# Two weight units multiplied side by side while the input arrives, a zeroed tile multiplied first, and index queries for positions 128 to 511 only

## The chip, the cores and the metric

The kernel runs on one core of a Trainium2 chip. The metric is the device time of one execution in microseconds, as the median of several runs. One execution was also recorded by the hardware profiler, and all rows below come from that one.

## What is computed

A decoder trunk of two layers over one sequence of 512 positions and 1024 features, in float32. Cut to what matters for the change, which sits in the first stage of the first layer:

```python
h = x @ w_in                                 # one combined projection
q_a, c_kv, q_idx, k_idx, w_idx, q_b, k_b, v_b, f_in = _split(h, EVEN_WIDTHS)
q_idx = q_idx.reshape(bsz, seq, 8, 64) * (64 ** -0.5)
log_f = log_sigmoid(f_in + b_f); cum_f = jnp.cumsum(log_f, axis=1)
# per block of 128 query positions:
idx = jnp.einsum('bthd,bsd->bths', qi, k_idx)
score = jnp.einsum('bth,bths->bts', wi, relu(idx))
score = jnp.where(causal, score, -inf)
_, sel = lax.top_k(score, k_sel)             # k_sel = 128 keys for each query
# 8 sparse heads attend to the chosen keys, 8 forgetting heads to all earlier keys;
# then output projection, norm, ConvFFN, norm; a second layer of another kind follows
```

A query at position t sees only the keys up to t, so the first 128 positions choose among at most 128 keys and need no scores.

## The kernel before

**Numbers.** Every float32 operand of a product is held as two float32r parts, `hi` and `lo`, whose sum is the float32 value: ScalarE (ACT) casts it to `hi`, VectorE (DVE) subtracts to get `lo`. A product is then three matmuls (`mm3`, lines 147 to 151): hi by hi, hi by lo, lo by hi.

**Weights.** They stream from DRAM in the order of use as 192 units of [128, 1024], 512 KB each (class `Stream`, lines 41 to 88). SyncE (SP) issues the loads into three `raw` buffers; line 75 casts on ACT and line 76 subtracts on DVE into one of three `whi`/`wlo` pairs, or into a `quad` tile where one is registered. `get(i)` also splits the two units that follow. A `raw` buffer is loaded again only after line 76 has read it, and a `whi`/`wlo` pair is written again only after the last matmul that reads it.

**The first stage.** `xq` holds the transposed input as eight pieces k of [128, 512]. Lines 121 to 134 load weight unit 0 whole, then the eight pieces of 256 KB each, and cut every piece (lines 130 and 131). Unit 0 (index keys, forget gates, index weights) is multiplied with `proj` (line 341): 8 pieces by 3 matmuls of 512 columns, 24 in all. Its evacuation on ACT and DVE follows, with the forget gates behind it (lines 343 to 359). Units 1 to 4 give the index queries (lines 364 to 369): 24 matmuls of 512 columns each, and two cuts per unit on 64 partitions. Unit 5 gives the latent keys (line 381).

**Scores and choice.** `scores(j)` for j = 1, 2, 3 (lines 410 to 426) multiplies the query columns from 128 on with the index keys: 48 matmuls, each pair followed by a Relu on ACT and an accumulation into `sel[j]` on DVE. The rounds that choose 128 keys (`choose`, lines 428 to 441) are 48 DVE rounds of MAX8 and MATCH_REPLACE8. Manual dependencies place them behind certain DVE instructions, so they are spread over the value projection (lines 452 to 457), the pairs of forgetting heads and the heads themselves. Their last result, line 440 for j = 3, goes through GpSimd (POOL, line 441 and lines 526 to 537) into the biases of the sparse heads.

**Order.** The kernel is written with a tile framework whose planner orders each engine's instructions by dependencies and by a modelled time, not strictly by the program text. For instance the split of unit 3 stands on ACT ahead of line 343.

## Time and profile before

| | us |
|---|---|
| median of 3 runs | 1188.16 |
| lowest and highest run | 1186.97, 1189.46 |
| span of the profiled execution | 1186.8 |
| TensorE matmul (PE) busy in the span | 1164.2 (98%) |
| DVE busy | 720.6 (61%) |
| ACT busy | 472.3 (40%) |

The profiled execution's own time is its span of 1186.8 us and what lies around it, the start and the end of the program; the median of the runs is 1.4 us above the span, and that difference is carried over unchanged. A PE busy share says little by itself, because matmuls overlap: their starts are closer together than their durations. The distance between starts is what is read below.

### The profile page before, as it was taken

How to read it: one execution, taken by the hardware profiler on the slowest of the kernel's cores; microseconds unless marked ns; L12 is line 12 of the kernel's file. 1: busy time of each engine (PE TensorE's matmuls, PEld its weight loads, DVE VectorE, ACT ScalarE, POOL GpSimd, SP SyncE). 2: the span in 40 equal slices, each digit the busy share in tenths (PEclk: the TensorE clock that was granted, in tenths of full speed). 3: DMA queues.
4: the chain of work that ended last, by engine and by line, in shares of the span. 5: the costliest groups of instructions: out<-in, count | busy, mean ns of one | idle time of the engine just before them, and what ended most of it. 6: DMA issues, size and time to landing. Idle time of an engine off the chain costs nothing. (4 is left out here: it accounts for less than half of the span.)

```text
span 1186.8 us, 14493 instructions
## 1 busy us (share of the span) xinstructions
PE 1164.2 (98%) x5512; PEld 966.4 (81%) x5512; DVE 720.6 (61%) x1216; ACT 472.3 (40%) x749; POOL 151.8 (13%) x238
## 2 busy tenths in 40 slices
PE   7999999899999999999999999999999999999997
PEld 6887777788988888888888788888888888888885
DVE  6889987847565656552236864466655666552226
ACT  6616666732434344441233342232444443432121
POOL 1033634203000000000002300003000000010003
PEclk9999998999999999999999999999999999999999
DMA  6633201242123232343344223471232323344221
GB/s 220 206 93 128 89 9 46 95 137 89 54 93 103 91 105 89 107 142 121 128 142 135 87 89 118 137 242 72 71 107 89 102 93 97 116 142 142 89 89 71
DMA packets 39685, 129.89 MB, mean 109 GB/s; under 512 B 5096, under 2 KB 5104, under 8 KB 39616
## 3 DMA queue, kind: packets, MB, share of 16 engines
q1 hardware_dynamic: 34560, 113.26, 29.0%
q0 software_dynamic: 5056, 15.71, 4.1%
q8 instruction: 43, 0.70, 0.3%
q14 instruction: 26, 0.21, 0.1%
HBM read 120.54 MB, written 9.99 MB: 110 GB/s over the span
## 5 line engine op out<-in xcount | busy, mean ns | idle before, releaser
L76 DVE TENSOR_TENSOR wlo<-raw,whi 128x1024 fp32r<-128x1024 f32 x161 | 197.3, 1226 | 290.7 <-ACT whi L75 289.6
L149 PE MATMUL bank<-quad,whi 128*128 128x512 f32 (+1 forms) x932 | 356.6, 383 | 6.3 <-ACT quad L130 6.3
L150 PE MATMUL bank<-quad,whi 128*128 128x512 f32 (+1 forms) x932 | 355.8, 382 | 0.5 <-DVE quad L131 0.5
L151 PE MATMUL bank<-quad,wlo 128*128 128x512 f32 (+1 forms) x932 | 355.9, 382 | 0.0
L75 ACT CAST whi<-raw 128x1024 fp32r<-128x1024 f32 x161 | 169.5, 1053 | 261.7 <-PE bank L151 120.6
L149 PEld LDWEIGHTS bank<-quad,whi 128*128 128x128 f32 x932 | 175.5, 189 | 40.2 <-ACT quad L130 6.3
L150 PEld LDWEIGHTS bank<-quad,whi 128*128 128x128 f32 x932 | 175.8, 189 | 34.6 <-DVE quad L131 1.1
L151 PEld LDWEIGHTS bank<-quad,wlo 128*128 128x128 f32 x932 | 175.7, 188 | 33.8
L150 PE MATMUL bank<-wlo,quad 128*128 128x512 f32 x388 | 151.0, 389 | 0.0
L151 PE MATMUL bank<-whi,quad 128*128 128x512 f32 x388 | 150.7, 389 | 0.0
L149 PE MATMUL bank<-whi,quad 128*128 128x512 f32 x388 | 149.5, 389 | 0.0
L149 PE MATMUL bank<-quad 128*128 128x512 f32 (+5 forms) x280 | 99.8, 360 | 0.5 <-ACT quad L187 0.5
L150 PE MATMUL bank<-quad 128*128 128x512 f32 (+5 forms) x280 | 98.7, 353 | 0.6 <-DVE quad L76 0.6
L151 PE MATMUL bank<-quad 128*128 128x512 f32 (+5 forms) x280 | 98.6, 353 | 0.0
L206 POOL DMA_DIRECT2D temp<-x x24 | 13.2, 549 | 567.9 <-ACT quadx L317 424.6
L150 PEld LDWEIGHTS bank<-wlo,quad 128*128 128x128 f32 x388 | 72.8, 188 | 15.2
L149 PEld LDWEIGHTS bank<-whi,quad 128*128 128x128 f32 x388 | 72.8, 188 | 15.1
L151 PEld LDWEIGHTS bank<-whi,quad 128*128 128x128 f32 x388 | 72.8, 188 | 14.9
L286 DVE SCALAR_TENSOR_TENSOR temp<-bank,fcw,temp 128x511 f32<-128x511 f32 x88 | 65.5, 744 | 9.1 <-ACT temp L285 9.1
L288 DVE SCALAR_TENSOR_TENSOR temp<-bank,fcw,temp 128x510 f32<-128x510 f32 x88 | 65.9, 748 | 3.0
L285 ACT ACTIVATE temp<-bank,fcw 128x512 f32<-128x512 f32 x88 | 59.9, 681 | 10.8 <-PE bank L151 10.8
L313 ACT ACTIVATE temp<-temp 128x512 f32<-128x512 f32 x44 | 27.8, 632 | 88.5 <-DVE temp L288 88.5
(143 smaller groups left out, 1274.2 us busy)
## 6 DMA issues: line engine op xcount, KB each, us to landing
raw<-in_ws_dram SPq DMA_DIRECT2D x192, 512.0 KB, 3.5
x<-temp SPq DMA_DIRECT2D x24, 256.0 KB, 2.0
temp<-x POOLq DMA_DIRECT2D x24, 256.0 KB, 3.2
temp<-in_xT_dram SPq DMA_DIRECT2D x8, 256.0 KB, 6.0
temp<-fk_d SPq DMA_DIRECT2D x8, 256.0 KB, 4.8
temp<-in_x_dram POOLq DMA_DIRECT2D x8, 256.0 KB, 3.1
quad<-in_ln_g_dram POOLq DMA_DIRECT2D x4, 512.0 KB, 5.2
quad<-in_ln_b_dram POOLq DMA_DIRECT2D x4, 512.0 KB, 6.6
```

Of the source, the lines that this page charges most:

```text
L75: nc.scalar.copy(hi, t)
L76: dve[0] = nc.vector.tensor_tensor(out=lo, in0=t, in1=_f(hi), op=ALU.subtract)
L149: nc.tensor.matmul(out, a[0], b[0], start=first, stop=False)
L150: nc.tensor.matmul(out, a[0], b[1], start=False, stop=False)
L151: return nc.tensor.matmul(out, a[1], b[0], start=False, stop=last)
L206: nc.gpsimd.dma_start(t, src[n * 128:n * 128 + 128, hf * 512:hf * 512 + 512])
L285: nc.scalar.mul(t, p, cw[:, j, 2:3])
L286: nc.vector.scalar_tensor_tensor(out=t[:, 1:], in0=p[:, :S - 1], scalar=cw[:, j, 1:2], in1=t[:, 1:], op0=ALU.mult, op1=ALU.add)
L288: nc.vector.scalar_tensor_tensor(out=t[:, 2:], in0=p[:, :S - 2], scalar=cw[:, j, 0:1], in1=t[:, 2:], op0=ALU.mult, op1=ALU.add)
L313: nc.scalar.activation(tg, tg, AF.Silu)
```

## The change

- A quad `misc` is taken first, and DVE sets its first [128, 512] part to zero. TensorE begins with 7 matmuls of 512 columns on that zero tile, whose result nobody reads (`WARM`).
- Units 0 and 1 are loaded directly, each in two halves of 256 KB (`load_w`), in among the eight input pieces: unit 0 first half, piece 0, unit 1 first half, pieces 1 to 3, unit 0 second half, piece 4, unit 1 second half, pieces 5 to 7. Each half is cut by itself.
- The two units are multiplied together, piece by piece: for each k three matmuls of unit 0 (512 columns) and three of unit 1.
- The index queries (units 1 to 4) are computed for columns 128 to 511 only: matmuls of 384 columns instead of 512, and cuts of 384 columns.
- Later units run through `Stream` as before. The evacuation of unit 0 with the gates follows the joint products, and the call that splits units 2, 3 and 4 stands in the program text behind it.

```diff
+    misc = quad()
     xq = [[quad(), quad()], [quad(), quad()]]
-    ws.load_to(1)
+    nc.vector.memset(_f(misc[:, 0]), 0.0)
+    w0 = [(rawp.tile([128, 1024], F32, name="raw"), wp.tile([128, 1024], FR, name="whi"),
+           wp.tile([128, 1024], FR, name="wlo")) for _ in range(FIRST)]
+    def load_w(u, hf):
+        c = slice(hf * 512, hf * 512 + 512)
+        raw, hi, lo = (t[:, c] for t in w0[u])
+        nc.sync.dma_start(raw, A["ws"][u][:, c])
+        nc.scalar.copy(hi, raw)
+        nc.vector.tensor_tensor(out=lo, in0=raw, in1=_f(hi), op=ALU.subtract)
...
+    load_w(0, 0)
+    load_x(0)
+    load_w(1, 0)
+    for k in (1, 2, 3):
+        load_x(k)
+    load_w(0, 1)
+    load_x(4)
+    load_w(1, 1)
+    for k in (5, 6, 7):
+        load_x(k)
+    ws.loaded = ws.split_to = base[0] = FIRST
...
-        misc = quad()
-        w = unit()
-        p = proj(w, xq)
+        q = bank()
+        for _ in range(WARM):
+            nc.tensor.matmul(q, misc[:, 0, :128], misc[:, 0], start=True, stop=True)
+        p0 = [bank() for _ in range(FIRST)]
+        for k in range(8):
+            for u in range(FIRST):
+                a = 128 if u else 0
+                w = w0[u][1:]
+                mm3(p0[u][:, a:], wk(w, k * 128, k * 128 + 128), xk(xq, k, a), k == 0, k == 7)
+        p = p0[0]
...
+        late_q = slice(128, S)
         for m in range(4):
-            p = proj(unit(), xq)
+            if m < FIRST - 1:
+                p = p0[1 + m]
+            else:
+                p = bank()
+                half(unit(), xq, p, 128, S)
             for s, (a, b) in enumerate(((slice(0, 64), slice(64, 128)), (slice(64, 128), slice(0, 64)))):
-                nc.scalar.mul(qi[s][a, m], p[a], float(HD ** -0.5))
+                nc.scalar.mul(qi[s][a, m, late_q], p[a, late_q], float(HD ** -0.5))
...
```

## Rows read from the trace of the kernel before

**Rows 1.** The page: the span, and the busy time, share and instructions of four engine rows (PE matmuls, PEld weight loads).

```profile
span 1186.8 us, 14493 instructions
...
PE 1164.2 (98%) x5512; PEld 966.4 (81%) x5512; DVE 720.6 (61%) x1216; ACT 472.3 (40%) x749; POOL 151.8 (13%) x238
```

**Rows 2.** The waits of TensorE over the whole run: who waited for whom, total us, times, longest us. The four longest.

```profile
PE bank L149 <- ACT quad L130: 6.3, 1, 6.3
PE bank L149 <- ACT pt L187: 3.5, 4, 1.4
PE bank L150 <- DVE pt L188: 1.2, 1, 1.2
PE bank L600 <- DVE d L590: 1.1, 1, 1.1
```

**Rows 3.** The timeline of TensorE from 0 to 52 us: start us, duration us. The first product, three at the first pitch, the first at another pitch, the first product of unit 1 and of unit 2, and the first scores.

```profile
6.34 0.80 PE L149 MATMUL bank<-quad,whi 128*128 128x512 f32 x1 [6.34 <-ACT quad L130]
...
8.27 0.63 PE L151 MATMUL bank<-quad,wlo 128*128 128x512 f32 x1
...
8.70 0.63 PE L149 MATMUL bank<-quad,whi 128*128 128x512 f32 x1
...
11.26 0.54 PE L149 MATMUL bank<-quad,whi 128*128 128x512 f32 x1
...
14.82 0.39 PE L149 MATMUL bank<-quad,whi 128*128 128x512 f32 x1
...
20.28 0.39 PE L149 MATMUL bank<-quad,whi 128*128 128x512 f32 x1
...
43.67 8.62 PE L416 MATMUL bank<-quad 128*128 128x256 f32 x48
```

**Rows 4.** The timeline of SP and ACT from 0 to 40 us: the issue of unit 0's load on SP; on ACT unit 0's cast, the casts of the input pieces (8 in three groups), the casts of units 2 and 3, the evacuation of unit 0 and the last instruction of its gates.

```profile
0.80 0.39 SPq L59 DMA_DIRECT2D raw<-in_ws_dram  x1
...
4.72 1.04 ACT L75 CAST whi<-raw 128x1024 fp32r<-128x1024 f32 x1 [2.64 <-DMA raw<-in_ws_dram]
5.67 1.13 ACT L130 CAST quad<-temp 128x512 fp32r<-128x512 f32 x2
...
10.17 1.96 ACT L130 CAST quad<-temp 128x512 fp32r<-128x512 f32 x3 [0.25 <-DMA temp<-in_xT_dram]
...
14.07 1.06 ACT L75 CAST whi<-raw 128x1024 fp32r<-128x1024 f32 x1 [0.23 <-DMA raw<-in_ws_dram]
15.63 1.06 ACT L75 CAST whi<-raw 128x1024 fp32r<-128x1024 f32 x1 [0.51 <-DMA raw<-in_ws_dram]
16.59 0.57 ACT L343 COPY temp<-bank 128x512 f32<-128x512 f32 x1
...
21.23 0.63 ACT L354 ACTIVATE temp<-temp 8x512 f32<-8x512 f32 x1
```

**Rows 5.** The timeline of DVE from 0 to 40 us: its last instruction before the input arrives, two groups of input cuts, the cut of unit 3, the first cut of unit 0's result, and a memset of 512 columns.

```profile
0.90 0.07 DVE L143 MEMSET mhalf<- 128x8 f32 x1
...
6.94 1.29 DVE L131 TENSOR_TENSOR quad<-temp,quad 128x512 fp32r<-128x512 f32 x2
...
10.83 2.04 DVE L131 TENSOR_TENSOR quad<-temp,quad 128x512 fp32r<-128x512 f32 x3 [0.17 <-ACT quad L130]
...
16.72 1.23 DVE L76 TENSOR_TENSOR wlo<-raw,whi 128x1024 fp32r<-128x1024 f32 x1 [0.34 <-ACT whi L75]
17.87 0.68 DVE L345 TENSOR_TENSOR quad<-bank,quad 64x512 fp32r<-64x512 f32 x1
...
22.74 0.48 DVE L356 MEMSET temp<- 8x512 f32 x1 [0.16 <-DVE temp L355]
```

**Rows 6.** The timeline of TensorE in the heads' stage, where matmuls of 384 columns stand in a row: the first of three, and the first of 512 columns behind them.

```profile
113.49 0.34 PE L149 MATMUL bank<-quad 64*128 64x384 f32 x1
...
114.02 0.39 PE L149 MATMUL bank<-quad 64*128 64x512 f32 x1
```

**Rows 7.** Busy time by stretch, all engines: start and end in us, length, busy us of PE, PEld, DVE, ACT, POOL with instruction counts, granted clock, DMA share, GB/s. The first two lines are two stretches of the input's loading (pieces of 2 KB a partition, then whole units of 4 KB), the next two the stretches up to and through the choice of keys, the last two the stretches at a low granted clock.

```profile
6.00:10.00 4.00, 3.12 (x7) 2.13 (x8) 3.55 (x6) 2.62 (x5) 0.00 (x0) 1.00 1.03 349
11.00:13.50 2.50, 2.50 (x12) 2.04 (x11) 1.86 (x3) 1.79 (x3) 0.00 (x0) 1.00 1.03 418
...
16.70:80.40 63.70, 63.70 (x294) 52.79 (x293) 52.39 (x103) 32.79 (x59) 11.65 (x25) 1.00 0.45 148
80.40:183.50 103.10, 103.10 (x538) 81.59 (x538) 95.77 (x251) 62.04 (x154) 40.36 (x84) 1.00 0.25 82
...
192.20:199.00 6.80, 6.80 (x27) 5.36 (x26) 4.63 (x16) 3.50 (x12) 1.59 (x3) 0.52 0.15 60
236.60:240.00 3.40, 3.40 (x17) 3.18 (x16) 1.98 (x3) 1.71 (x2) 0.00 (x0) 0.54 0.47 158
```

**Rows 8.** The instructions of DVE from 15 to 45 us by line and shape (count, busy us, mean ns, idle before them), the line that cuts the index queries.

```profile
L368 DVE SCALAR_TENSOR_TENSOR quad<-bank,quad 64x512 fp32r<-64x512 f32 x8 | 5.5, 689 | 1.5 <-ACT quad L367 1.3
```

**Rows 9.** The instructions of line 440, the last comparison of each choice of keys: their durations in ns, first and last start in us.

```profile
L440 DVE TENSOR_TENSOR sel<-temp,sel x3: 424/540/693, 79.2 to 183.5; 128x256 f32<-128x256 f32 x1, 128x384 f32<-128x384 f32 x1, 128x512 f32<-128x512 f32 x1
```

**Rows 10.** The waits from 178 to 202 us: who waited for whom, total us, times, longest us.

```profile
POOL sel L441 <- DVE sel L440: 6.3, 1, 6.3
...
DVE d L572 <- POOL d L535: 2.1, 2, 1.6
```

More of the change, by code (lines that the diff above doesn't have):

```diff
@@ L31 @@
 S1, S2, S3, S4 = 4, 3, 1, 2
+WARM = 7
 def _f(ap):
@@ L118, in unit, with load_x @@
         return ws.get(i)
+    FIRST = 2
+    misc = quad()
     xq = [[quad(), quad()], [quad(), quad()]]
-    ws.load_to(1)
-    def load_x(c):
-        for j in range(2):
-            r = temp()
-            k = 2 * c + j
-            nc.sync.dma_start(r, A["xT"][:, k])
-            hi, lo = xq[0][k // 4][:, k % 4], xq[1][k // 4][:, k % 4]
-            nc.scalar.copy(hi, r)
-            nc.vector.tensor_tensor(out=lo, in0=r, in1=_f(hi), op=ALU.subtract)
-    for c in range(4):
-        load_x(c)
+    nc.vector.memset(_f(misc[:, 0]), 0.0)
[7 more added lines that the diff above has]
+        nc.vector.tensor_tensor(out=lo, in0=raw, in1=_f(hi), op=ALU.subtract)
+    def load_x(k):
+        r = temp()
+        nc.sync.dma_start(r, A["xT"][:, k])
+        hi, lo = xq[0][k // 4][:, k % 4], xq[1][k // 4][:, k % 4]
+        nc.scalar.copy(hi, r)
+        nc.vector.tensor_tensor(out=lo, in0=r, in1=_f(hi), op=ALU.subtract)
+    load_w(0, 0)
[9 more added lines that the diff above has]
+    ws.loaded = ws.split_to = base[0] = FIRST
     ident = cst.tile([128, 128], F32)
@@ L359, in _body @@
         nc.gpsimd.dma_start(fk_d, cw[g])
-        for k in range(5, 9):
-            ws.big[base[0] + k] = quad
+        for k in range(6, 10):
+            ws.big[k] = quad
         qi = [quad(), quad()]
+        late_q = slice(128, S)
         for m in range(4):
-            p = proj(unit(), xq)
+            if m < FIRST - 1:
[3 more added lines that the diff above has]
+                half(unit(), xq, p, 128, S)
             for s, (a, b) in enumerate(((slice(0, 64), slice(64, 128)), (slice(64, 128), slice(0, 64)))):
-                nc.scalar.mul(qi[s][a, m], p[a], float(HD ** -0.5))
-                nc.vector.scalar_tensor_tensor(out=qi[s][b, m], in0=p[a], scalar=float(HD ** -0.5),
-                                               in1=_f(qi[s][a, m]), op0=ALU.mult, op1=ALU.subtract)
+                nc.scalar.mul(qi[s][a, m, late_q], p[a, late_q], float(HD ** -0.5))
+                nc.vector.scalar_tensor_tensor(out=qi[s][b, m, late_q], in0=p[a, late_q], scalar=float(HD ** -0.5),
+                                               in1=_f(qi[s][a, m, late_q]), op0=ALU.mult, op1=ALU.subtract)
         p = bank()
```

## The prediction

> **What bounds the kernel now.** I read the page first: TensorE's matmuls are busy 98% of a span of 1186.8 us, DVE 61%, ACT 40% [rows 1]. Overlapping matmuls make such a share too kind, so I read TensorE's waits next: the largest is 6.3 us, once, for the first input piece, and the next three come to 5.8 us together [rows 2]. So TensorE seldom waits, and what it is spared early should reach the end, unless another engine then comes last.
>
> The starts of its matmuls give the price of a product. Unit 1's first product starts at 14.82 and unit 2's at 20.28 [rows 3]: 24 products of 512 columns in 5.46 us, 0.2275 us each, which is little over 512 columns at 2.4 GHz (0.213). The first products were slower: 8.27 to 8.70 is 0.43 us, 512 columns at 1.2 GHz, and the distance changes only in the product that starts at 11.26 [rows 3]. The engine began at 6.34 and was fed without a gap from 8.27. So the first stage has three losses: TensorE has nothing until 6.34, runs at half speed until 11.3, and spends 5.46 us on each index-query unit, a quarter of it on columns that no score reads.
>
> The third reading is the choice of keys. Its last comparison starts at 183.5 [rows 9]; POOL waits 6.3 us for it, DVE 2.1 us for POOL [rows 10], and TensorE 1.1 us for DVE [rows 2], and a stretch at a granted clock of about half follows, 6.8 us long [rows 7]. From 80.4 to 183.5 DVE is busy 95.77 of 103.1 us, 93% [rows 7]. So DVE's stream is the second bound, and it is nearly as tight as TensorE's.
>
> **Part 1: the joint start.** The arrival of data decides first. Unit 0, 512 KB, was there at 4.72; the last group of three pieces began to be cast at 10.17 and took 1.96 us [rows 4], so the last piece was there by 11.5. Its lo part was done at 12.87 [rows 5]. The pieces, 2 KB a partition, moved at 349 GB/s [rows 7]. With 256 KB first, the first half of unit 0 is there about 0.75 us sooner, at 4.0; piece 0 follows 0.75 us later, at about 4.9 with the queue, and its cast takes some 0.6 us (two in 1.13) [rows 4]. First product at 5.5, the second 0.7 us later (the lo cut, two in 1.29 us [rows 5]). Piece 7 has 512 KB more ahead of it, 1.3 to 1.5 us at 418 or 349 GB/s [rows 7]: there at 12.8, cast by 13.4, cut by 14.1.
>
> The work for TensorE is 24 products at 0.2275 and 24 of 384 columns. For the latter the nearest rows are those of the heads: three in a row from 113.49 to 114.02, 0.177 us each, on 64 rows [rows 6]; in proportion to 512 columns it is 0.171. I take 0.174. Together 5.46 + 4.18 = 9.6 us, 1.2 us per piece, against an arrival of 0.75 us per transfer and twelve transfers: from the second product on TensorE is the later one. At full clock: 6.2 + 9.4 = 15.6, and 0.2 for the cold part: 15.8. The arrival alone would allow 14.1 plus five products, 15.0.
>
> The clock: the zeroed tile takes DVE one memset, 0.48 us for 512 columns [rows 5], from about 0.95, so the seven products can start at 1.45 and last 7 x 0.43 = 3.0 us, to 4.5. Nothing in the trace shows how much of that counts. Before, the clock rose 4.9 us after the first product of any kind [rows 3]; the same distance from 1.45 gives 6.4. The bounds: at once at 4.5, or as if there had been no zero products, 5.5 + 4.9 = 10.4. In the second case some 4.4 us of work run at half speed, 2.2 us lost. So the joint products end at 15.7 to 17.9, I take 16.0, where unit 2 began at 20.28: **4.3 us** earlier (2.4 to 4.6). The memset and the zero products themselves lie in time in which both engines had nothing; they cost nothing as long as they end before 5.5.
>
> A rule of the Trainium skill speaks against the halves: DMA: Bandwidth & Descriptors, Bandwidth, asks for transfers of 1 MiB or more, because each carries a fixed cost. By its table such a load would reach between 32% (64 KB) and 78% (1 MB) of the peak, and the sum would be that of the rival of the fixed part, below. The trace disagrees so far: pieces of just this size followed each other at 349 GB/s [rows 7], so I keep the 0.75 us.
>
> **Part 2: narrower queries.** Units 2, 3 and 4 have 72 products, each shorter by 0.2275 - 0.174 = 0.0535 us: **3.8 us**. The bounds are 0.171 and 0.177 a product [rows 6]: 3.6 to 4.1 us. Each of the eight DVE cuts of 0.689 us [rows 8] loses a quarter of its columns, by an estimate in proportion to the columns 0.14 us each, 1.1 us; the same holds on ACT.
>
> The Trainium skill (Perfetto Trace Analysis, Identifying the Most-Contended Engine) says that matmul busy time tells little about TensorE, and to go by the share of weight loads. Here that share is 81% [rows 1], which would leave a fifth as headroom, and shorter products might bring nothing (a sum of 1185.3); the distance between starts, 0.2275 where the columns need 0.213, says that they do, and I go by it.
>
> **Part 3: who is late next.** The scores would begin 4.3 + 3.8 = 8.1 us earlier, at 35.6. Three things could hold that back. First, the split of unit 3, which needs the pair of unit 0 and so cannot be hoisted ahead of the joint products' end. It was on ACT at 15.63, ahead of the evacuation [rows 4]. If it stays ahead, its cast is done by about 17 and TensorE, which needs it at 20.2, does not see it. Unit 2's load follows piece 7 (512 KB, 1.3 us: 14.1, as in [rows 4]) and needs no freed pair. The SP queue carries twelve issues instead of nine ahead of it, and they are issued long before the data move.
>
> Second, the evacuation of unit 0 does not come earlier: its products now end about 1 us later than 14.82. DVE's list from unit 3's cut at 16.72 on [rows 5] thus starts at the same time, though TensorE then needs its end 8 us sooner. It held 52.39 us of work in 63.7 us up to 80.4, 82% [rows 7]. With 1.1 us less work and the 93% density that DVE reaches later [rows 7], the list ends at 16.7 + 55.2 = 71.9, 8.5 us earlier: no loss. At the old 82% it is 1.3 us earlier: nearly all is lost. Nothing shows the density it will reach; the work is ready earlier, and eight temporaries and eight banks keep TensorE from seeing a lag at once, so I take 90%, near the upper end: 57.0 us, 6.7 us earlier.
>
> Third, the last comparison ends DVE's chain [rows 9], so past 183.5 DVE's shift and not TensorE's is what counts. That takes **1.4 us** off (0 to 6.8). Behind it, TensorE has no long waits left in the run [rows 2], and a shift is simply kept.
>
> **Sum:** 1186.8 - 4.3 - 3.8 + 1.4 = 1180.1 us of span. What lies around the span is not touched; the median of the runs is 1.4 above it, so 1188.2 - 6.7 = **1181.5 us**. About 0.2% (2.4 us) is what a measurement of this kernel can tell from no change.
>
> **The rivals.**
>
> *Late start or late split* (1184.0). The zero products do not raise the clock, or unit 3's cast is planned behind the gates, whose last ACT instruction came 4.6 us after the first [rows 4]: cast and cut would then be ready 2 to 3 us after TensorE wants them. Either costs some 2.5 us. For it: nothing shows that zero products raise the clock. Against: the split stood ahead before.
>
> *DVE keeps its pace* (1186.9). Its list up to 80.4 takes the old 82%, so the choice ends 1.3 us earlier and TensorE waits for it at about 188. For it: DVE's gaps there are partly its own chains through ACT. Against: much of the gap is waiting for products that now come sooner.
>
> *Slower: more waits at half clock* (1192). TensorE, 8 us ahead of a DVE that is not, waits not in one place but in several between 100 and 240. Waits of some 1 us there [rows 2] were followed by 6.8 and 3.4 us at half clock [rows 7]: 3.4 and 1.7 us lost. Two more stretches of the longer kind on top of the DVE case (1186.9 + 6.8 = 1193.7; one and a short one, 1192) make the change a loss. It decides from the point where DVE's shift is under 1 us. Against: the planner fills with projections until 188.
>
> *Each half load pays its fixed part* (1186.5). 512 KB took 3.9 us from its issue at 0.80 to its cast at 4.72 [rows 4], of which 1.5 are data at 349 GB/s. If each of the three extra transfers added the other 2.4 us, piece 7 would be there at 20.0, the joint products would end at 21, 0.7 us later than before; of the 3.8 us less 1.4, 1.7 us remain. This is the skill's rule at work; the pace of the pieces speaks against it.
>
> *Better* (1178.1). The longer stretch at half clock goes with the wait ahead of it: 6.7 + 3.4 us.
>
> **How the numbers follow.** Forecast 0.56, late start or split 0.18, DVE's pace 0.12, slower 0.07, fixed part 0.03, better 0.04. The likeliest, 1181.5, has its own range of 1179.5 to 1183.5 from the bounds of parts 1 and 2. The wider range of 1177.0 to 1186.8 takes in the late start and the better case, and leaves out the slower case and about the upper half of DVE's. Faster by over 0.2% (below 1185.8) are the forecast, the late start, the better case and a little of the others: 0.82; within 0.2%: 0.11; slower: 0.07.
>
> **What would show it.** First real product at 5.5, distance 0.23 from about 6.4, unit 2's first product at 16.0, its distance 0.174, scores at 35.6, the last comparison at about 177, the same waits behind it. Wrong would be: half speed beyond 8 us, a TensorE wait on line 75 or 76 near 20 us, or a TensorE wait at the heads that was not there before.

## The result and the profile after

The changed kernel takes 1195.33 us (median of 5 runs, 1192.33 to 1197.41), the kernel before 1188.63 in the same comparison: ratio 1.0057, interval 1.0043 to 1.0071. It is slower by 6.7 us, where 6.7 us less were forecast; 1195.3 lies outside the range. The profiled execution has a span of 1193.5 us (its time 1195.23) against 1186.8.

The waits of TensorE over the whole run (who waited for whom, total us, times, longest us), against [rows 2]:

```profile
PE bank L405 <- DVE temp L384: 5.9, 1, 5.9
PE bank L168 <- ACT pt L206: 5.7, 3, 3.4
```

The old longest wait, 6.3 us for the first piece, is gone. In its place stands one nearly as long that was not there at all: line 405, the four transposes that bring the forget gates' sums into the columns for the biases, waits for line 384, the scan that forms these sums (357 before). The second line was 3.5 us.

The timeline of TensorE at its start, against [rows 3]:

```profile
1.51 3.35 PE L361 MATMUL bank<-quad 128*128 128x512 f32 x7 [1.51 <-DVE mhalf L162]
5.17 0.51 PE L168 MATMUL bank<-quad,whi 128*128 128x512 f32 x1 [0.31 <-ACT quad L140]
7.57 0.44 PE L168 MATMUL bank<-quad,whi 128*128 128x384 f32 x1 [1.89 <-ACT whi L133]
7.84 0.39 PE L169 MATMUL bank<-quad,whi 128*128 128x512 f32 x1
...
9.11 0.79 PE L168 MATMUL bank<-quad,whi 128*128 128x512 f32 x1 [0.45 <-ACT quad L140]
...
11.83 0.61 PE L168 MATMUL bank<-quad,whi 128*128 128x512 f32 x2
...
19.30 0.34 PE L168 MATMUL bank<-quad,whi 128*128 128x384 f32 x1
```

The first real product comes at 5.17 and the pace at 7.84 is the full one, as forecast. But TensorE waits 1.89 us for the second unit's first half and 0.45 us for piece 1; from 9.11 to 11.83 the products of 512 columns are 0.43 us apart again, and unit 2 starts at 19.30 where 16.0 was forecast and 20.28 stood before.

The same timeline where the queries end and the scores begin: the last query product, the transposes, the first latent-key product, the first of them at full pace, the scores.

```profile
31.61 0.34 PE L170 MATMUL bank<-quad,wlo 128*128 128x384 f32 x1
37.83 1.08 PE L405 MATMUL bank<-ident,temp 128*128 128x128 f32 x4 [5.88 <-DVE temp L384]
38.56 0.78 PE L168 MATMUL bank<-quad,whi 128*128 128x512 f32 x1
...
42.55 0.44 PE L168 MATMUL bank<-quad,whi 128*128 128x512 f32 x1
...
47.15 1.09 PE L448 MATMUL bank<-quad 128*128 128x256 f32 x7
```

TensorE is through with the queries at 31.95, where the transposes began at 36.60 before: 4.65 us ahead. It loses 5.88 us in the wait and runs at half pace from 38.56 to 42.55 (granted clock 0.50 from 36.0 to 42.6, below), so the latent keys take 7.54 us (38.56 to 46.10) instead of 24 times 0.2275, 5.46. The scores start 3.5 us later than before [rows 3] instead of 8.1 earlier.

Why the scan is late is read on ACT and DVE. The chain is copy (370), ACT (378), DVE (379), ACT exponential (380), ACT logarithm (381), DVE (382), DVE memset (383), scan (384). The timeline of ACT, then that of DVE:

```profile
19.86 0.57 ACT L370 COPY temp<-bank 128x512 f32<-128x512 f32 x1
...
22.27 0.72 ACT L378 ACTIVATE temp<-temp,bf 8x512 f32<-8x512 f32 x1
...
25.64 1.04 ACT L76 CAST quad<-raw 128x1024 fp32r<-128x1024 f32 x1
26.70 0.63 ACT L380 ACTIVATE temp<-temp 8x512 f32<-8x512 f32 x1
...
30.48 0.63 ACT L381 ACTIVATE temp<-temp 8x512 f32<-8x512 f32 x1
```

```profile
24.02 0.68 DVE L379 SCALAR_TENSOR_TENSOR temp<-temp 8x512 f32<-8x512 f32 x1
...
31.14 0.68 DVE L382 SCALAR_TENSOR_TENSOR temp<-temp 8x512 f32<-8x512 f32 x1 [0.64 <-ACT temp L381]
...
32.72 1.23 DVE L77 TENSOR_TENSOR quad<-raw,quad 128x1024 fp32r<-128x1024 f32 x1 [0.31 <-ACT quad L76]
34.10 0.48 DVE L383 MEMSET temp<- 8x512 f32 x1 [0.16 <-DVE quad L77]
34.62 1.23 DVE L77 TENSOR_TENSOR quad<-raw,quad 128x1024 fp32r<-128x1024 f32 x1
...
36.47 1.22 DVE L384 TENSOR_TENSOR_SCAN temp<-temp 8x512 f32<-8x512 f32 x1
```

From the copy at 19.86 to the scan's end at 37.69 are 17.8 us. The durations of the eight steps add up to 5.6 us, and ACT loads a table for 1.28 us ahead of the logarithm: 6.9 us, the same as before. Between the steps stand casts and lo cuts of weight units (76, 77) and query cuts (399, 400). Before, the copy stood at 16.59 [rows 4] and the scan ended at 25.74, 9.1 us; the transposes behind it waited for nothing. The scan on DVE and the transposes on TensorE in the kernel before:

```profile
24.52 1.22 DVE L357 TENSOR_TENSOR_SCAN temp<-temp 8x512 f32<-8x512 f32 x1
```

```profile
36.60 0.60 PE L373 MATMUL bank<-ident,temp 128*128 128x128 f32 x4
```

Busy time by stretch (start and end, length, busy us of PE, PEld, DVE, ACT, POOL with counts, granted clock, DMA share, GB/s), first of the kernel before, then of the changed one:

```profile
20.00:30.00 10.00, 10.00 (x45) 8.27 (x45) 6.80 (x8) 6.73 (x8) 0.53 (x1) 1.00 0.31 112
```

```profile
6.00:8.00 2.00, 0.43 (x2) 0.44 (x3) 0.46 (x1) 0.62 (x1) 0.00 (x0) 1.00 0.88 206
...
20.00:30.00 10.00, 10.00 (x59) 10.00 (x59) 9.46 (x12) 9.55 (x14) 0.00 (x0) 1.00 0.64 201
...
36.00:42.60 6.60, 4.77 (x14) 3.93 (x15) 5.12 (x6) 1.81 (x4) 0.53 (x1) 0.50 0.64 215
...
243.60:250.40 6.80, 5.60 (x13) 4.44 (x14) 4.86 (x8) 3.98 (x7) 0.00 (x0) 0.53 0.48 154
```

Between 20 and 30 us DVE is busy 9.46 of 10 us instead of 6.80, and ACT 9.55 instead of 6.73, with weights arriving at 201 GB/s instead of 112. The work of later units came forward into the stretch that holds the gates' chain. The last line belongs to a second loss. The instructions of line 472 (440 before, [rows 9]), whose last start is the choice's end:

```profile
L472 DVE TENSOR_TENSOR sel<-temp,sel x3: 424/540/692, 82.7 to 187.0; 128x256 f32<-128x256 f32 x1, 128x384 f32<-128x384 f32 x1, 128x512 f32<-128x512 f32 x1
```

It is 3.5 us late, exactly the lateness of the scores. From there to the last head's last product are 68.4 us against 64.0, and from there to the end of the span 1.2 us less than before: 3.5 + 4.4 - 1.2 = 6.7. That last product before and in the changed kernel:

```profile
247.47 0.28 PE L151 MATMUL bank<-pt,quad 128*128 128x128 f32 x1
```

```profile
255.39 0.28 PE L170 MATMUL bank<-pt,quad 128*128 128x128 f32 x1
```

ACT and, behind it, TensorE at the last head:

```profile
241.51 1.04 ACT L76 CAST quad<-raw 128x1024 fp32r<-128x1024 f32 x1 [2.09 <-DMA raw<-in_ws_dram]
242.74 1.05 ACT L76 CAST quad<-raw 128x1024 fp32r<-128x1024 f32 x1 [0.19 <-DMA raw<-in_ws_dram]
```

```profile
244.80 0.79 PE L168 MATMUL bank<-pt,quad 128*128 128x512 f32 x1 [3.40 <-ACT pt L206]
```

Two casts of output-projection weights, which wait for their transfer, stand on ACT ahead of the last head's casts, the first of which starts at 244.17; TensorE waits 3.40 us, and from 243.6 to 250.4 the granted clock is about half (0.53, above).

### The profile page after: what moved, and what is told of

Its sections match the earlier page's. It is cut to its first block, busy times and chain, and to the rows that moved or that the text cites. A ratio compares the mean times of both kernels' runs of the same rounds, so it can differ in the third digit from the quotient of the medians.

```text
span 1193.5 us, 14505 instructions
## 1 busy us (share of the span) xinstructions
PE 1165.9 (98%) x5519; PEld 968.4 (81%) x5519; DVE 720.0 (60%) x1219; ACT 471.8 (40%) x751; POOL 152.1 (13%) x238
## 5 line engine op out<-in xcount | busy, mean ns | idle before, releaser
L77 DVE TENSOR_TENSOR wlo<-raw,whi 128x1024 fp32r<-128x1024 f32 x159 | 194.9, 1227 | 291.6 <-ACT whi L76 290.8
L168 PE MATMUL bank<-quad,whi 128*128 128x512 f32 (+2 forms) x932 | 354.7, 382 | 2.6 <-ACT whi L133 1.9
L170 PE MATMUL bank<-quad,wlo 128*128 128x512 f32 (+2 forms) x932 | 354.8, 381 | 0.0
L169 PE MATMUL bank<-quad,whi 128*128 128x512 f32 (+2 forms) x932 | 354.3, 380 | 0.0
```

The costliest lines, as they stand in the source:

```text
L77: dve[0] = nc.vector.tensor_tensor(out=lo, in0=t, in1=_f(hi), op=ALU.subtract)
L168: nc.tensor.matmul(out, a[0], b[0], start=first, stop=False)
L169: nc.tensor.matmul(out, a[0], b[1], start=False, stop=False)
L170: return nc.tensor.matmul(out, a[1], b[0], start=False, stop=last)
```

## The experiments

Each was timed beside the kernel before, whose medians were 1188.5 to 1188.8. The executions of one kernel lie 2 to 7 us apart, and a trace is one of them (e12's lies 1.1 us below its median, e5's 1.3 above), so a difference of 1 us between two experiments, in the times or in the traces, proves nothing by itself. Theory: TensorE's queue was stopped at the transposes by the gates' chain, which the planner had stretched with weight work, and all else follows. The rival from the prediction: DVE's total work up to the choice is the second bound. The short name at the head of each is used below.

**e1, transposes moved back.** The block of transposes with its two casts stands behind the latent-key products.

```diff
-        p = bank()
-        for n in range(NCH):
-            nc.tensor.transpose(p[:, n * 128:n * 128 + 128], cw[:, n * 128:n * 128 + 128], ident)
...
         p = proj(unit(), xq)
         cut2(misc[:, 2], misc[:, 3], p)
         c_hi, c_lo = misc[:, 2], misc[:, 3]
+        p = bank()
+        for n in range(NCH):
+            nc.tensor.transpose(p[:, n * 128:n * 128 + 128], cw[:, n * 128:n * 128 + 128], ident)
...
```

> The changed kernel with one move: the four transposes that read the gates' scan, and the two small ACT instructions behind them, stand behind the latent-key products instead of ahead of them. Theory G (TensorE stands in its own queue behind the transposes until DVE's scan is done, 5.9 us, and the latent-key products behind it then run at half speed, 2.0 us more): the long wait goes, the scores start 7 to 8 us earlier (near 39 to 40 instead of 47.15), and the time falls from 1195.3 to 1187.5 to 1190, as DVE had 5.8 us of idle time there to give. Theory H (the loss lies in the order that the planner gave to the heads' stage, not in the first stage): the scores start earlier but the heads' end stays where it is, and the time stays within 1 us of 1195.

1185.53 us, ratio 0.9975 (0.9965 to 0.9985): 9.8 us faster than the changed kernel, and faster than the one before. Its timeline of TensorE:

```profile
37.31 0.63 PE L410 MATMUL bank<-ident,temp 128*128 128x128 f32 x4 [0.36 <-DVE temp L384]
...
38.92 0.97 PE L448 MATMUL bank<-quad 128*128 128x256 f32 x6
40.88 0.47 PE L448 MATMUL bank<-quad 128*128 128x256 f32 x2 [0.98 <-DVE quad L400]
41.64 9.30 PE L448 MATMUL bank<-quad 128*128 128x256 f32 x40 [0.29 <-ACT wi L415]
50.78 0.39 PE L168 MATMUL bank<-quad 128*128 128x512 f32 x1
```

The wait is down to 0.36 us although the scan starts at 35.95, nearly as late as before the edit: the transposes, now behind the latent-key products, come that much later. The loss at the last head is gone as well (choice's end 182.1, heads' end 245.3: 63.2 us). Of the 9.3 us between the two traces 4.9 lie before the choice's end and 5.2 at the heads, with 0.8 lost behind them; so more than half of the gain stands where theory H looked, though the edit is in the first stage. But the scores, 4.75 us early, stop twice and run at half clock from 42.0 to 45.3 (granted 0.50); the value projection, the first product behind them, is only 1.35 us early (52.13 before).

**e5, gates pinned.** Here the transposes stay, and the casts and cuts of units 5 to 9 are ordered behind the gates' logarithm and scan.

```diff
-        nc.scalar.copy(hi, t)
+        c = nc.scalar.copy(hi, t)
...
+        if 5 <= i < 10:
+            self.tc.add_manual_dep(c.ins, pin[0].ins.name, AFTER, ...)       # the gates' Ln
+            self.tc.add_manual_dep(dve[0].ins, pin[1].ins.name, AFTER, ...)  # the gates' scan
```

> The changed kernel with its transposes where they were, ahead of the latent-key products, but with the casts (ACT) and lo cuts (DVE) of weight units 5 to 9 ordered behind the gates' Ln and scan. In the changed kernel the scan started at 36.47, 16.6 us after the first ACT instruction of unit 0's evacuation (19.86), and TensorE waited 5.88 us for it. Theory 'interleaved work': the casts and cuts between the gates' steps stretch the chain; without them the scan starts about 9 us after the evacuation, near 29, the wait at the transposes goes to under 0.5 us, and the time is near that of the transposes moved back: 1184 to 1187 us. Rival 'the chain is long by itself' (hand-overs between ACT and DVE): the scan stays past 34, the wait stays over 3 us, 1192 to 1195. Second rival 'the wait only moves': the scan is early but unit 5's cut, now late, keeps TensorE waiting 2 to 5 us ahead of the latent-key products, 1188 to 1192.

1186.61 us, 0.9981 (0.9971 to 0.9990): 8.7 us faster than the changed kernel by order alone. DVE's and TensorE's timelines:

```profile
27.99 1.22 DVE L390 TENSOR_TENSOR_SCAN temp<-temp 8x512 f32<-8x512 f32 x1
```

```profile
31.08 0.60 PE L411 MATMUL bank<-ident,temp 128*128 128x128 f32 x4
...
41.89 0.78 PE L454 MATMUL bank<-quad 128*128 128x256 f32 x4 [1.86 <-ACT far L436]
```

With the copy at 19.16 the scan ends after 10.1 us, and the transposes wait for nothing. So the chain is not long by itself, as the first theory expected; the interleaved weight work made it 17.8 us. The stop in the scores comes here too, 1.86 us, for another small instruction on ACT, queued behind a weight cast.

**e2, e3, e4: parts of the change alone.** e2 is the kernel before with the queries for columns 128 to 511 alone, e3 the changed kernel without zero products, e4 the changed kernel with all 512 columns.

```diff
e2:  -            p = proj(unit(), xq)
     +            p = bank()
     +            half(unit(), xq, p, 128, S)
e3:  -WARM = 7
     +WARM = 0
e4:  -                a = 128 if u else 0
     +                a = 0
     -        late_q = slice(128, S)
     +        late_q = slice(0, S)
```

> The kernel before with the index queries for columns 128 to 511 only, and nothing else of the change. Theory G: with unit 0 done at 14.8 as before, the scan is done near 26, TensorE reaches the transposes at 31.5 and waits for nothing; 96 products shorter by 0.054 us give 5.2 us, some of which DVE's list may not follow: 1183 to 1186. Theory H (any earlier arrival at the heads is lost in DVE's chain): 1187 to 1189, no change.

> The changed kernel with no products on the zero tile (WARM = 0). Theory G: the zero products bring little, since the clock that they raise falls again in the gap behind them; the first products run at half speed until about 9 to 11, the joint products end 0 to 1.5 us later, the wait for the scan shrinks by as much, and the time stays within 2 us of 1195. Rival Z (the zero products disturb the start: clock up, down and up again, and this is what makes the change slow): 1190 or less.

> The changed kernel with all 512 columns in the index queries again: the joint start alone. Theory G: TensorE reaches the transposes some 5 us later, near 36.5, so the wait for the scan shrinks from 5.9 to 1 or 2 us and what follows runs at full speed: the time stays near 1192 to 1195 although 5.2 us of products are added. Theory H: the added products are simply added, 1199 to 1201.

e2: 1187.04 us, 0.9992 (0.9982 to 1.0003), not told apart from the kernel before and short of the 1183 to 1186 of theory G. Its transposes wait for nothing and the scores start at 38.96, 4.7 us earlier; then TensorE waits 1.91 us for line 399 on ACT, half clock follows, and at the choice (182.5) 1 us is left.

e3: 1192.03 us, 1.0031 (1.0019 to 1.0043). The wait at the transposes is 5.5 us, and the choice ends only 1.2 us sooner than in the changed kernel; the loss at the last head is absent (64.6 us from the choice's end to the heads' end). Unit 2 starts at 18.54. In the six traces that share the changed kernel's start (that one, e1, e5, e9, e12, e15) it starts between 18.59 and 19.53, so no gain and no cost of the seven zero products stands out.

e4: 1190.12 us (1185.34 to 1191.39), 1.0005 (0.9993 to 1.0017), 5.2 us faster than the changed kernel although its queries have a third more columns. Its row for the transposes:

```profile
37.53 0.63 PE L405 MATMUL bank<-ident,temp 128*128 128x128 f32 x4 [0.76 <-DVE temp L384]
```

The scan starts at 36.16, within 0.3 us of the changed kernel. TensorE simply arrives later with the longer products and waits 0.76 us instead of 5.88. What the narrower queries save up to the transposes went into this wait and the half clock that followed: the choice ends at 184.4, 2.6 us sooner than in the changed kernel. Another 3.9 us are the loss at the last head, which e4 does not have (64.5 us).

**e10, e11, e7: the start** (each on top of e1). e10 loads units 0 and 1 whole, e11 has 14 zero products, e7 lets unit 1 follow unit 0 by three pieces.

```diff
e10: -    load_w(0, 0)
     +    load_w(0)
          load_x(0)
     -    load_w(1, 0)
     -    for k in (1, 2, 3):
     +    load_w(1)
     +    for k in range(1, 8):
              load_x(k)
e11: -WARM = 7
     +WARM = 14
e7:  +        for i in range(11):
     +            for u, k in ((0, i), (1, i - 3)):
```

> The changed kernel with transposes behind the latent-key products (as in e1, 1185.5), but units 0 and 1 loaded whole, in the order unit 0, piece 0, unit 1, pieces 1 to 7. In e1 as in the changed kernel the DMA engines moved 150 to 275 GB/s between 6 and 8 us, against 335 to 371 before, the second unit's first half was cast at 6.9 and the last piece at 14.4. Theory 'the half loads cost transfer rate': whole loads keep 335 GB/s or more, the last piece is cast by 13.5, and although the first product starts 1 us later, unit 2 starts within 0.5 us of e1's 18.8: 1185 to 1186.2. Rival 'halves pay': the first product and the clock come later, unit 2 starts at 20 or later, and 1186.5 to 1188 results.

> The changed kernel with transposes behind the latent-key products (as in e1, 1185.5) and 14 zero products instead of 7, so that TensorE is busy until about 7.3, when the second unit's first half arrives. In e1 as in the changed kernel the zero products ended at 4.8, TensorE waited 2.0 us for that half, and 0.43 us a product held from about 8.2 to 11.2. Theory 'the wait behind the zero products lost the clock': with the gap filled the products stay at 0.23 from 7.5 on and unit 2 starts at 16.8 to 17.6 instead of 18.8. Rival 'arrival decides': the later pieces hold TensorE, unit 2 starts at 18.3 or later. Of the time, if the list of casts and cuts is the second bound, nothing: 1185 to 1186; if TensorE's start counts, 1184.

> The changed kernel with transposes behind the latent-key products (as in e1, 1185.5), and the joint products staggered: unit 1 follows unit 0 by three pieces, so unit 0's sum is complete about 2.5 us earlier, while the joint products end where they did. Theory 'DVE's list starts with unit 0's evacuation and is the second bound': evacuation and gates start 2 to 3 us sooner, and the choice of keys ends 1 to 3 us sooner than e1's 182.1: 1182.5 to 1184.5. Rival 'that list is held by what TensorE hands it, not by its start': the choice ends within 0.5 us of e1's, 1185 to 1186. Rival on the other side: unit 0's products with nothing between them wait for each arriving piece, the clock falls, the joint products end 1 us later than 19, 1186 to 1187.

e10: 1187.09 us, 0.9985 (0.9976 to 0.9994), 1.6 us slower than e1. DMA moves 369 GB/s from 6 to 8 us (206 in the changed kernel, 314 in e1, so the 150 to 275 of the expectation fit the changed kernel alone) and the last pieces are cast by 13.5 (15.0 in the changed kernel, 14.2 in e1), but the first product comes at 6.08, the second unit's at 8.85, and unit 2 at 19.66 against e1's 18.82. Since starts of the same kind scatter from 18.59 to 19.53, it is not shown that halves pay at this place. The time difference, whose intervals overlap, does not come from the start, since the choice ends 1.1 us sooner than in e1.

e11: 1187.47 us, 0.9996 (0.9986 to 1.0007). TensorE's timeline and one stretch:

```profile
1.51 5.64 PE L361 MATMUL bank<-quad 128*128 128x512 f32 x14 [1.51 <-DVE mhalf L162]
...
7.62 0.40 PE L169 MATMUL bank<-quad,whi 128*128 128x512 f32 x1
```

```profile
8.00:10.00 2.00, 1.93 (x10) 1.21 (x9) 1.39 (x3) 1.69 (x3) 0.00 (x0) 1.00 1.04 387
```

The gap before the second unit's half is filled, the granted clock stays at 1.00 (e1 in this stretch: 0.50), and unit 2 starts at 17.56, 1.26 us sooner than in e1, within what the first theory expected. The choice ends 1.2 us sooner (180.9). In e13, with the same 14, unit 2 starts at 17.55: this is clear of the scatter. And still the kernel is 1.9 us slower than e1: the heads behind the choice take 64.7 us instead of 63.2, and behind the heads its trace loses 1.8 us more; why is not shown.

e7: 1185.64 us, 0.9976 (0.9966 to 0.9985). Unit 0's copy comes only 0.42 us sooner (18.97 for 19.39), not 2 to 3, and the choice ends 0.3 us sooner. The edit did not do what it was made for, so it says nothing about the list.

**e9, e12, e13, e14, e16: the lists in front of the scores.** e9 (on e1) puts the lo cuts of units 6 to 9 on POOL. e12 (on e1) orders the casts and cuts of units 10 to 12, first used some 22 us after the scores, behind the Relus and accumulations of the second key block. e13 is e12 with 14 zero products, e16 e12 with none. e14 is the kernel before with narrow queries, late transposes and e12's order, so without halves, zero products or joint products.

```diff
e9:  +        if 6 <= i < 10:
     +            nc.gpsimd.tensor_tensor(out=lo, in0=t, in1=_f(hi), op=ALU.subtract)
e12: +        if 10 <= i < 13:
     +            self.tc.add_manual_dep(c.ins, pin["act"].ins.name, AFTER, ...)       # last Relu, j = 2
     +            self.tc.add_manual_dep(dve[0].ins, pin["dve"].ins.name, AFTER, ...)  # its accumulation
```

> The changed kernel with transposes behind the latent-key products (as in e1, 1185.5), and the lo cuts of weight units 6 to 9 on POOL instead of DVE: four cuts of 128x1024, some 4.9 us of DVE's work between about 22 and 60 us. Theory 'DVE's list is the second bound': v_b starts 2 to 4 us sooner than e1's 50.8, the choice ends near 178.5 to 180 in place of 182.1, and 1182 to 1184 results. Rival 'DVE's list is not tight, its gaps wait for ACT and TensorE': the choice ends within 1 us of e1's, 1184.5 to 1186. Rival on the other side: POOL takes over twice as long for a cut as DVE, the raw buffers come free late, and TensorE waits for a unit's cut between 40 and 60 us: 1187 to 1190.

> The changed kernel with transposes behind the latent-key products (as in e1, 1185.5), and with the casts and lo cuts of weight units 10, 11 and 12 ordered behind the scores' Relu and accumulations of the second key block. They are first used some 22 us after the scores end; in e1 two of the cuts stood on DVE (37.8 to 40.1) ahead of the last index-query cut, for which the scores waited 0.98 us, and a cast stood on ACT ahead of the index weights (0.29 us), with a stretch at half clock behind. Theory 'the order of DVE's and ACT's lists in front of the scores is the second bound': the scores run through without a wait, v_b starts 2 to 3 us sooner than e1's 50.8, the choice ends at 179 to 180.5 in place of 182.1, 1182 to 1184. Rival 'the amount of work on DVE is the bound': the cuts are paid behind the scores, the choice ends within 0.6 us of 182.1, 1185 to 1186. Rival on the other side: the three raw buffers stay full, the stream of weights stands still for 15 us and TensorE waits for a later unit: 1187 or more.

> The doubled zero products and the pinned later units together. If both theories hold (clock kept at the start, lists free in front of the scores), TensorE's 1.5 us at the start reach the scores as well: scores 1 to 1.5 us sooner than with the pinned units alone, and 1181 to 1183. If the scores then wait for the query cuts again, the time is that of the pinned units alone within 0.5 us.

> The kernel before with index queries of 384 columns, transposes behind the latent-key products and units 10 to 12 pinned behind the scores, but without zero products, half loads or joint products. It shows what the joint start is worth when neither the transposes' wait nor the lists in front of the scores hold TensorE. Unit 2 starts at 20.3 less 0.05 x 24 = 19.0, which is within 0.3 us of e1's 18.8. Theory 'the joint start gives next to nothing here': within 1 us of the kernel with the pinned units alone. Rival 'it gives the difference of the first product': over 1.5 us slower than that.

> The kernel of e12 (transposes behind the latent-key products, units 10 to 12 behind the scores; 1185.65) without the zero products. Taking the seven zero products from the changed kernel let unit 2 start 0.76 us sooner (18.54 for 19.30). If they cost as much here, the scores start 0.5 to 0.9 us sooner than e12's 39.72 and the time is 1184.5 to 1185.5. Rival: the heads behind the choice give it back, as they did with the doubled zero products, where scores 1.1 us sooner ended in a time 1.9 us later: 1186 to 1187.5.

e9: 1188.71 us, 0.9998 (0.9990 to 1.0007), 3.2 us slower than e1. Timelines of DVE, POOL and ACT:

```profile
32.78 2.93 DVE L387 TENSOR_TENSOR_SCAN temp<-temp 8x512 f32<-8x512 f32 x1
```

```profile
32.22 2.41 POOL L78 TENSOR_TENSOR quad<-raw,quad 128x1024 fp32r<-128x1024 f32 x1 [1.15 <-ACT quad L76]
```

```profile
44.02 1.04 ACT L76 CAST whi<-raw 128x1024 fp32r<-128x1024 f32 x1 [2.61 <-DMA raw<-in_ws_dram]
```

A cut takes 2.4 us on POOL (1.23 on DVE), it slows DVE beside it, and a cast on ACT waits 2.61 us for its transfer, ahead of the scores' Relus: TensorE stops 2.47 us, and the choice ends at 185.1. The rival on the other side was right in its first and last step; that the transfer is late because POOL frees its buffer late is argued, not shown.

e12: 1185.65 us, 0.9974 (0.9965 to 0.9983). Its scores on TensorE:

```profile
39.72 8.62 PE L454 MATMUL bank<-quad 128*128 128x256 f32 x48
49.05 0.50 PE L174 MATMUL bank<-quad 128*128 128x512 f32 x1 [0.71 <-ACT temp L456]
```

They run through in one group, at the old 8.62 us, without a wait; a stop of 0.71 us, for a Relu behind the casts that were moved there, stands after them. The value projection starts at 49.05, 1.7 us sooner than in e1, and the choice ends at 180.5. That is the order theory, at 1.7 us where 2 to 3 were expected. Yet the median is e1's within 0.1 us, not the 1182 to 1184 of that theory: the order is shown in the trace, a gain in time is not.

e13: 1187.08 us, 0.9990 (0.9982 to 0.9999): scores 1.4 us sooner than e12's, the value projection 0.16 us sooner, the choice 0.15 us; the heads take 65.2 us. The 1.4 us were lost in the scores, which took 10.16 us instead of 8.62: TensorE had waited 1.00 us at the transposes ahead of them, and from 38 to 42 us the granted clock was 0.59 and 0.55. Neither expected time came.

e16: 1185.31 us, 0.9974 (0.9964 to 0.9984): unit 2 at 18.96, within the scatter of e3, scores at 38.88, choice at 179.7; heads 65.1 us. Without zero products the time is the same.

e14: 1185.89 us, 0.9978 (0.9968 to 0.9988). The first product of unit 1 and that of unit 2:

```profile
15.12 0.33 PE L155 MATMUL bank<-quad,whi 128*128 128x384 f32 x1
...
19.31 0.33 PE L155 MATMUL bank<-quad,whi 128*128 128x384 f32 x1
```

Without anything of the joint start unit 2 begins at 19.31; in the changed kernel it began at 19.30. The time is e12's within 0.3 us.

**e15, the last head.** The changed kernel with only ACT's order at the last head altered.

```diff
-SEQ = ("LBT3S3VN", "LBT2S3VN")
+SEQ = ("LBT3S3VN", "LBT2S3VN", "LBST23VN")   # the last for h == 15
...
+            c = nc.scalar.copy(hi, p)
+            if pin:
+                tc.add_manual_dep(c.ins, pin[0].ins.name, AFTER, ...)   # pt of head 14 behind the exponentials of head 15
```

> The changed kernel with nothing altered at its start. Only at the last head ACT's order is set: the four exponentials of head 15 stand ahead of the three pt casts of head 14, as they do in the kernels without the loss there (with the transposes moved, without the zero products, with all 512 columns); in the changed kernel the fourth exponential stood behind two of these casts. In the changed kernel TensorE then waited 3.40 us for the last head's pt at 244.80 and half clock held from 243.6 to 250.4; between the choice's end (187.0) and the heads' end (255.4) lay 68.4 us, against 64.0 before. Theory 'ACT's order at the last head': 64 to 65 us between them, the heads end near 251.5, 1191 to 1192. Rival 'it follows from where the heads stand against the weight loads, not from that order': the wait stays at 2.5 us or more and 1194 to 1195.5 results. The start should not differ: 5.9 us of wait at the transposes in both.

1192.60 us, 1.0032 (1.0020 to 1.0044): 2.7 us faster than the changed kernel, with the transposes' wait as it was (6.0 us). From the choice's end (187.63) to the heads' end (253.25) are 65.6 us instead of 68.4. TensorE at the last head:

```profile
245.91 0.50 PE L169 MATMUL bank<-pt,quad 128*128 128x512 f32 x1 [2.77 <-ACT pt L207]
```

So the order on ACT accounts for some 2.7 of the 4.4 us (the two intervals just touch): the stretch at half clock of 6.8 us is no longer there. Both expectations came in part: the heads take less, though not the 64 to 65 us of the theory, and the wait itself stays at 2.77 us, a sign of the rival, whose time did not come. The waits for pt together grew from 5.7 to 6.8 us. Two weight casts, the first late by 2.27 us for its transfer, still stand on ACT ahead of these casts; that the other 1.7 us come from them is not shown.

## Why the prediction was wrong

**The step that failed** is "who is late next" in Part 3. It names three things that could hold back the scores: unit 3's split, the evacuation with DVE's list behind it, the last comparison. What held them back was a fourth, the forget gates' chain into the transposes. These stand in TensorE's queue ahead of 24 latent-key products and of the scores, which do not need them. The rows to see it were there: the evacuation at 16.59 and the gates' last ACT step [rows 4], and transposes that waited for nothing at 36.60. I read those only as "no long wait". The slack was 36.60 less the scan's end at 25.74, 10.9 us, and the change spent it from both ends: TensorE 4.65 us earlier, the chain 3.3 us later at its start and 8.7 us longer, 16.6 in all; less the slack that is 5.8, and the wait measured 5.88. By e5, e1 and e4 this is shown three ways: shorten the chain, move the waiting instruction out of the way, or let TensorE arrive later, and the wait goes (none, 0.36 and 0.76 us) and the choice ends 5.1, 4.9 and 2.6 us sooner. This is the 3.5 us at the choice; the 4.4 us at the heads are a second step, below.

**The chain's length** could not be taken from the trace of before, where it took 9.1 us. Even 8.1 us earlier, at 28.5, TensorE would have met a chain of that length (copy near 17.6 by the forecast, scan done at 26.7) without waiting. The forecast failed because I moved casts and cuts in time without asking which other instructions they would then stand between.

**The start: 4.3 us forecast, 1.0 measured.** "From the second product on TensorE is the later one" failed at the second product: the second unit's half was cast at 6.89 and TensorE waited 1.89 us. In the changed kernel's trace the zero products did raise the clock (without them, in e3, the products at this place begin 0.43 us apart), but two waits later the pace was half again for 2.7 us; in e9, e12 and e15, with the same start, the pace was half from the first real products on. e11 shows this second cause by itself: 1.26 us. e14 shows the sum: the joint start, halves and zero products together gained nothing at unit 2 that stands out of the scatter (18.59 to 19.53 against 19.31). In the changed kernel's trace the 1.0 us is what unit 1's narrower products bring without any of them: 24 times 0.0535 is 1.3, less the 0.3 by which e14 began unit 1 later (15.12 for 14.82). The rival of the late start had a price near this, 2.5 us, but for a clock that does not rise or a late split; unit 3's split stood in time.

**The narrower queries: 3.8 us forecast, 3.84 measured.** 72 products took 12.48 us (19.30 to 31.78, 0.1733 each) instead of 16.32. The Trainium skill (Perfetto Trace Analysis, Identifying the Most-Contended Engine) would have had TensorE's headroom read from the share of weight loads; here the distance between starts decided, as the prediction took it. The weight loads filled 10.00 of 10 us between 20 and 30 in the changed kernel, and the products kept that distance. The cuts too lost the 0.14 us each that the prediction gives (0.55 for 0.69), though its working does not lead there: a quarter of 0.689 is 0.17.

**DVE as the second bound: wrong.** In all sixteen traces, that of the kernel before among them, 131.3 to 131.5 us lie between the value projection's first product and the choice's end (before 52.13 to 183.5; e14 48.18 to 179.7; the changed kernel 55.61 to 187.0). None of them lists a wait of TensorE in that stretch up to 181 us. So DVE, at its 93% [rows 7], kept up with the products, for starts from 4 us sooner to 4 us later. So the 1.4 us of Part 3 and the rival of DVE's pace were built on the wrong stretch. The limit was in front of it, between 20 and 50 us, and not of amount but of order: a query cut, an index-weight cast or a far-bias cast behind weight work that nobody needed yet. e12 shows that for the scores: same work, other order, no stop in them.

**The slower rival** gave 1192 through more waits followed by half clock. The signature is right (a wait and some 6.8 us at about half clock with it, twice), but its place and cause are not: it put them on a DVE that lags between 100 and 240 us and gave them 7%.

**Behind the choice: "a shift is simply kept".** It is not. The heads from 183 to 250 us take 62.9 to 66.3 us in all kernels but one (64.0 before, 68.4 in the changed kernel), with no plain order by their arrival: the eight earliest take 64.7 us in the mean, and so do the eight latest. e11 and e13 lost there what they had gained. For the changed kernel e15 gives 2.7 of 4.4 us to ACT's order at the last head. What decides the rest, and why some kernels take 63 us there and others 65, is open.

A version that beats both kernels is e1 (1185.53, 0.25% below the kernel before); e7, e12, e14 and e16 do the same with more edits or fewer, within 0.4 us.

Of the signs that the prediction named, the first product (5.17 for 5.5), the distance of 0.174 and a full pace before 8 us came; the starts of unit 2, of the scores and the choice's end did not, and two of its three signs of failure did: half speed beyond 8 us, and a new wait at the heads (3.40).

## What to carry to other kernels

When an engine is to be spared time, list every instruction in its own queue for the next stage and look up when each operand is ready, also for those that wait for nothing now: their slack is the most that the saving can be, and work that comes forward on the other engines can eat it from the other side. An instruction that waits for a long chain, and whose result is wanted late, belongs behind the work that does not need it: here that one move was worth 9.8 us, about half of it in front of the choice and the other half at the heads, where it was not looked for. Where a planner orders the queues, an edit to one stage may change the order in another, so compare the orders before believing a saving.

## What the runs showed of the hardware

Seven zero products did not hold the clock. In all nine traces with seven of them TensorE then waited 0.8 to 2.1 us for the second unit's first data. In six the products began at the full distance and fell to the half one by 9.2 us (changed kernel: granted clock 0.62 and then 0.52 from 8 to 12 us). In three, e9, e12 and e15, the first products behind that wait stood 0.43 us apart from the start. With 14 and no such wait (e11, e13) the distance stayed at 0.23 and the granted clock at 1.00. The granted clock does not tell the slow start: it reads 1.00 in e12 from 6 to 10 us, and [rows 7] before from 6 to 10 us, while products of 512 columns stand 0.43 us apart. From e12's timeline of TensorE:

```profile
7.47 0.63 PE L175 MATMUL bank<-quad,whi 128*128 128x512 f32 x1
7.90 0.63 PE L176 MATMUL bank<-quad,wlo 128*128 128x512 f32 x1
```

A lo cut on POOL held up DVE's scan: it started at 32.78 beside a POOL cut that ran from 32.22 to 34.63, and took 2.93 us where it takes 1.22 alone, so it ended 1.08 us after POOL's cut. The Trainium skill (SBUF — State Buffer, Who interferes with whom) says that a DVE instruction with two SBUF inputs contends with a GpSimd one that reads SBUF, and that the port pair they share is an exclusive lock. These two rows agree with it.

Between 6 and 8 us half-unit loads among the pieces moved 206 GB/s in the changed kernel and 314 in e1, and 197 to 350 over all twelve traces that have them; whole loads moved 333 to 369 in four. From 8 to 12 us the changed kernel, e1 and e10 all moved 380 to 400. So in those 2 us the halves came more slowly as a rule; why is not shown, and unit 2 still began 0.84 us later with whole loads than in e1.
